# Three small reorderings in a float32 encoder kernel: a longer warm-up, low parts of probabilities last, and the last down-projection input split by parts

## The chip, the cores and the metric

The kernel runs on one core of a Trainium2 chip. The metric is device time in microseconds (us) of one execution; lower is better. The core's engines run at the same time and wait for each other through semaphores: TensorE (PE, matmuls into PSUM banks), VectorE (DVE), ScalarE (ACT), GpSimd (POOL), and the DMA queues, most of which SyncE (SP) issues. A matmul has a weight load (PEld) beside it.

## The reference, cut to what matters

A two-layer encoder over 512 tokens of width 1024 in float32. Layer 0 mixes tokens with gated linear attention, layer 1 with softmax attention; each is followed by a gated MLP of inner width 2816 with a width-3 convolution.

```python
def block(q_blk):
    s = jnp.einsum('bkgqd,bksd->bkgqs', q_blk, k).astype(jnp.float32) * scale
    p = jax.nn.softmax(s, axis=-1).astype(v.dtype)
    return jnp.einsum('bkgqs,bksd->bkgqd', p, v)

def conv_ffn(h, w_up, w_conv, b_conv, w_down):
    u = h @ w_up
    u = lax.conv_general_dilated(u, w_conv[:, None, :], window_strides=(1,), padding=[(1, 1)], ...) + b_conv
    val, gate = jnp.split(u, 2, axis=-1)
    return (jax.nn.silu(gate) * val) @ w_down

for i in range(DEPTH):
    h = rmsnorm(x, norm_mix[i])
    ...
    x = x + gla_mixer(h, ...)      # i = 0;  attn_mixer(h, ...) for i = 1
    x = x + conv_ffn(rmsnorm(x, norm_ffn[i]), ffn_w_up[i], ffn_w_conv[i], ffn_b_conv[i], ffn_w_down[i])
```

## The kernel before, in words

**Products in three parts.** TensorE multiplies in a rounded float32 format (fp32r). To keep float32 accuracy each operand is split into a high part (rounded by ScalarE, `activation(..., AF.Copy)`) and a low part (what rounding left, a subtraction on VectorE). A product is then three matmuls into one PSUM bank, in the helper `mm3(ps, wh, wl, mh, ml, ...)`: weight high by moving high, weight high by moving low, weight low by moving high. All matmuls go through `mm`, line 90 of the profile, so the profile tells them apart by the names of their tiles.

**Order of instructions.** A planner orders each engine's instructions ahead of time, by program order and its own estimate of when operands are ready; on the chip each engine then works its list in order and waits at semaphores. From the last block of an MLP's up-projection on (`pinned[0]`), the matmuls keep program order exactly. In the attention they do not: there the planner may put matmuls of one step between those of another.

**PSUM.** There are eight banks, in four groups that rotate: `acc` (3), `s` (2), `pt` (2), `po` (1). A tile that takes a bank waits until the last reader of the tile that had it is done.

**The start.** While the first weights and inputs are on their way, TensorE multiplies constants into a bank named `warm` (float32, 128 columns; each matmul leaves two records in the profile). Its first eight columns, all -0.5 after eight accumulated matmuls, are kept as `halfneg`. The first real matmuls are the tiles `vg`.

**Attention.** For each of 8 heads and each half of the queries (256), `turn` transposes two blocks of probabilities (tile `pt`, from `pr`) and splits them into `pth` (ScalarE) and `ptl` (VectorE). `mix` multiplies them with the values (`vh`, `vl`) for four blocks of keys into the bank `po`: twelve matmuls. The output projection (`op`, `out_stream`) and the next heads' query projections (`A`, `B`) are laid between the steps. `oT` is the split result of a head.

**The MLP's end.** The down-projection is done in six parts of the 22 inner blocks (`PARTS`, the last one of 3), each part adding into the residual `x` (line 900) one tile `dn` for each of the 8 row blocks of `x`. The inputs are the split gated activations `gu`: high at line 837 on ScalarE, low at line 838 on VectorE. The last part cannot end before the last `gu` is there, so its first tiles start early: each of 3 (first layer) or 4 (second layer) takes a bank from `LAST_BANKS` and multiplies its first two inputs, and only then comes the last input of each, with `finish`: the add into `x` and, in the first layer, the next norm's split of that row block (`xhl`, lines 357 and 362, and its square, 366 and 370), in the second the write to the output. The remaining tiles follow, one after the other, from bank `acc`. In the second layer the last row block ends in two halves, written by two queues (lines 889 to 895).

**Weights.** `Weights` converts weights ahead of their use into six buffers `w` (three pairs of high and low); a conversion waits until the last matmul that reads the old contents has passed. The first weights of the attention (`raw`, lines 171 and 173) are converted on ScalarE when a pair of the last down weights is free; their low part is finished by a DMA that adds (line 215). The first attention projection is the tile `A`, which reads `xhl` of all eight row blocks in order.

Of the kernel before, what the change touches and what calls it, by code (L numbers as in the profile page):

```python
# [15 lines left out]
P = 128  # L16
# [3 lines left out]
NT = S // P  # L20
# [3 lines left out]
QH, HD = 8, 128  # L24
# [21 lines left out]
FIRST_DMA = False  # L46
IN_TWO = ()
STEPS = 4
STEPS0 = 9
EARLY_INNER = (3,)  # L50
IN_BANKS = ("s", "s", "s", "acc")
AFTER = (False, False, False, True)
AT_TAG = 't'
LAST_BANKS = (("acc", "acc", "po"), ("acc", "acc", "s", "acc"))
SHARES1 = (2, 2, 2, 2)

PC_NORM = 0
# [7 lines left out]
def hybrid_encoder_kernel(  # L65
# [23 lines left out]
    def mm(*a, **k):  # L89
        i = pe.matmul(*a, **k)  # L90
        if pinned[0]:
            tc.keep_in_program_order(i)
# [13 lines left out]
    def bank(tag, n):  # L106
        return pp.tile([P, S], F32, tag=tag, bufs=PS[tag], name=nm(n))

    def pair(tag, bufs, dt, n):
        return sp.tile([P, 2 * S], dt, tag=tag, bufs=bufs, name=nm(n))  # L110

    def big(dt, n):
        return pair("g", 22, dt, n)
# [3 lines left out]
    def tmp(tag, n, w=S, dt=F32):  # L117
        pool_ = sp if tag == "sq" else stage[-1]
        return pool_.tile([P, w], dt, tag=tag, bufs={"u": 4, "t": 6, "sq": 3}[tag], name=nm(n))
# [183 lines left out]
    two = tmp("sq", "two")  # L303
    dve.memset(two[:, :P], 2.0 ** -5)
    dve.memset(two[:, P : 2 * P], -(2.0 ** -6))
    warm = bank("po", "warm")
    for i in range(8):
        mm(warm[:, :P], two[:, :P], two[:, P : 2 * P], start=i == 0, stop=i == 7)
    halfneg = cp.tile([P, 8], F32, name="halfneg")
    dve.tensor_copy(halfneg, warm[:, :8])  # L310
    ones = cp.tile([P, 1], F32, name="ones")
# [78 lines left out]
    def mm3(ps, wh, wl, mh, ml, start, stop, **k):  # L390

        mm(ps, wh, mh, start=start, stop=False, **k)
        mm(ps, wh, ml, start=False, stop=False, **k)
        mm(ps, wl, mh, start=False, stop=stop, **k)
# [368 lines left out]
    def ffn(layer, norm, cw, nxt):  # L763
        H = S // 2
        wide = lambda n: stage[-1].tile([P, 2 * S], F32, tag="w4", bufs=4, name=nm(n))
        hl, forms = [], {}
# [74 lines left out]
        def plain(m, part):  # L841
            u = wide("u")
            for t in range(2):
# [6 lines left out]
                elif m > 0:  # L850
                    for _ in range(STEPS):
                        next(building, None)
                if m == 0 and t == 1:
                    dve.tensor_tensor(u[:, :S], first, norm.R, ALU.mult)
                    dve.tensor_tensor(u[:, S:], ps, norm.R, ALU.mult)
                    for _ in range(STEPS0):
                        next(building, None)
# [41 lines left out]
        def finish(c, ps, last):  # L899
            dve.tensor_tensor(x[c], x[c], ps, ALU.add)  # L900
            if last and nxt is not None:
                nxt.chunk(c)
            elif last:
                sync.dma_start(out[c * P : (c + 1) * P, :], x[c])
# [48 lines left out]
        tiles = part_tiles(len(PARTS) - 1)  # L953
        k0, ends_ = sum(PARTS[:-1]), {}
        early = [(c, us, bank(tag, "dn")) for (c, us), tag in zip(tiles, LAST_BANKS[layer])]
        for late in (False, True):
            for c, us, ps in early:
                for i, u in enumerate(us):
                    if (i == len(us) - 1) != late:
                        continue  # L960
                    if u // 8 not in ends_:
                        ends_[u // 8] = W.half(down[layer], u // 8)
                    wh, wl = ends_[u // 8]
                    sl = slice((u % 8) * P, (u % 8 + 1) * P)
                    mm3(ps, wh[:, sl], wl[:, sl], *hl[k0 + i], i == 0, late)
                if late:
                    finish(c, ps, True)
        cur[0] = ends_[tiles[len(early) - 1][1][-1] // 8]
        for c, us in tiles[len(early):]:
# [3 lines left out]
    def attention(norm, nxt):  # L973
# [63 lines left out]
        def split(y, tile_):  # L1037
            act.activation(tile_[:, :S], y, AF.Copy)
            dve.tensor_tensor(tile_[:, S:], y, tile_[:, :S].bitcast(F32), ALU.subtract)
# [51 lines left out]
        ps = [bank("acc" if j < 2 else "pt", "av") for j in range(NT)]  # L1091
# [7 lines left out]
        vh, vl = big(F32R, "vh"), big(F32R, "vl")  # L1099
        for j in range(NT):  # L1100
            sl = slice(j * 256, (j + 1) * 256)
# [49 lines left out]
        def mix(h, hf):  # L1151
            ph3, pl3 = pts.pop((h, hf))
            vo = (h // 4) * HD
            if hf == 0:
                pos[h] = bank("po", "po")
            dst = pos[h][:, hf * 256 : (hf + 1) * 256]
            for k in range(NT):
                vsl = slice(k * 256 + vo, k * 256 + vo + HD)
                mm3(dst, vh[:, vsl], vl[:, vsl], ph3[:, k, :], pl3[:, k, :], k == 0, k == NT - 1)
            if hf == 1:  # L1160
                t = big(F32R, "oT") if h < 4 else pair("xhl", 8, F32R, "oT")
                split(pos[h], t)
                oh[h] = (t[:, :S], t[:, S:])
# [11 lines left out]
        for t in range(len(blocks) + LAG2):  # L1175
            if t < len(blocks):
                scores(*blocks[t])
            if 1 <= t <= len(blocks):
                copy(*blocks[t - 1])
            for g in plan[t]:  # L1180
                next(g, None)
            if LAG <= t < len(blocks) + LAG:
                turn(*blocks[t - LAG])
            if t < len(blocks):
                shares(*blocks[t])
            if t >= LAG2:
                h, j = blocks[t - LAG2]
                if j % 2 == 1:
                    mix(h, j // 2)
# [14 lines left out]
    with staged("ffn0"):  # L1204
        ffn(0, norms[1], cw, norms[2])
    with staged("att"):
        attention(norms[2], norms[3])
    with staged("ffn1"):
        ffn(1, norms[3], cw, None)
# [87 lines left out]
```

## Time and profile before

| | |
|---|---|
| median of 3 timed runs | 1103.08 us (1102.5, 1103.11, 1103.08) |
| the profiled execution's own time | 1100.86 us |
| its span, first to last instruction | 1099.1 us |
| TensorE busy | 1092.6 us (99%), 6530 matmul records |
| VectorE, ScalarE, GpSimd busy | 888.9 (81%), 620.2 (56%), 73.5 us (7%) |
| granted TensorE clock, mean of the span | 1.000 |

A row of the timeline gives the start in us, the busy time in us, the engine, the line, the operation, "out<-in", shapes and how many instructions were merged into the row (x2); in brackets stands how long the engine had been idle before it and who released it. Ends of matmuls are modelled, so the time that a matmul costs in a stream is read from the starts of its row and the next one, not from its duration. "Q" behind an engine (SPq) is its DMA issue.

### The profile page before, as it was taken

The numbers are of one execution on the slowest core, as the hardware profiler recorded it, in microseconds if no ns is written. First come the engines' busy times: TensorE is split into PE (matmuls) and PEld (weight loads), VectorE is DVE, ScalarE is ACT, GpSimd is POOL, SyncE is SP. The second block draws the span as 40 slices with busy tenths as digits, with TensorE's granted clock in tenths as the row PEclk, the third lists the DMA queues.
The fourth block names the chain that finished last, engine by engine and source line by source line (L and its number), as shares of the span: only waits on it lengthen the run. The fifth ranks groups of instructions, "written<-read, shape, count | busy, mean of one in ns | idle before, by whom it ended". The sixth has DMA issues, their size and how long they took to land.

```text
span 1099.1 us, 16431 instructions
## 1 busy us (share of the span) xinstructions
PE 1092.6 (99%) x6530; PEld 972.3 (88%) x6530; DVE 888.9 (81%) x1392; ACT 620.2 (56%) x913; POOL 73.5 (7%) x74
## 2 busy tenths in 40 slices
PE   9999999999999999999999999999999999999998
PEld 7888888888899999999988888888889999999997
DVE  6786675569999999979885567666999999997985
ACT  6478343467555545444464878956755454554441
POOL 0100000011000000000004334001100000000000
PEclk9999999999999999999999999999999999999999
DMA  6422221378323232323338754446733323232322
GB/s 223 148 93 77 77 100 65 118 163 191 123 104 116 96 116 77 126 69 113 124 91 201 180 161 122 159 146 163 189 120 111 116 96 115 78 121 72 116 77 77
DMA packets 31084, 132.72 MB, mean 121 GB/s; under 512 B 3616, under 2 KB 4128, under 8 KB 22304
## 3 DMA queue, kind: packets, MB, share of 16 engines
q1 hardware_dynamic: 20352, 102.16, 27.7%
q0 software_dynamic: 5184, 18.88, 8.9%
q10 hardware_dynamic: 5472, 10.64, 2.6%
q8 instruction: 51, 0.84, 0.3%
q14 instruction: 25, 0.20, 0.1%
HBM read 100.21 MB, written 2.10 MB: 93 GB/s over the span
## 4 chain that ended last, share of the span: by engine, by line
PE 93%; issue 3%; DMA 2%; DVE 1%; POOL 0%; ACT 0%; SPq 0%; POOLq 0%
PE dn L90 21%; PE Y L90 18%; PE X L90 13%; PE op L90 8%; PE vg L90 8%; PE up L90 5%; PE A L90 3%; PE B L90 3%; PE po L90 2%; PE s L90 2%; PE k L90 2%; PE q L90 2%; DMA wl<-raw 2%; PE o L90 1%; PE av L90 1%
## 5 line engine op out<-in xcount | busy, mean ns | idle before, releaser
L90 PE MATMUL dn<-gu,wh 128*128 128x512 f32 x708 | 218.6, 390 | 0.1
L90 PEld LDWEIGHTS dn<-gu,wh 128*128 128x128 f32 x708 | 130.3, 188 | 26.0 <-DVE x L900 1.0
L90 PE MATMUL dn<-gu,wl 128*128 128x512 f32 x354 | 137.4, 388 | 0.0
L830 ACT ACTIVATE y<-u,cw 128x512 f32<-128x512 f32 x88 | 67.8, 807 | 87.0 <-DVE u L934 75.0
L90 PE MATMUL X<-th,xwh 128*128 128x256 f32 x384 | 108.7, 283 | 0.0
L90 PE MATMUL X<-th,xwl 128*128 128x256 f32 x384 | 108.7, 283 | 0.0
L90 PE MATMUL X<-tl,xwh 128*128 128x256 f32 x384 | 108.7, 283 | 0.0
L171 ACT ACTIVATE wh<-raw 128x1024 fp32r<-128x1024 f32 x72 | 76.2, 1058 | 52.2 <-DVE raw L204 16.4
L90 PE MATMUL up<-xhl,wh 128*128 128x512 f32 x320 | 99.0, 390 | 0.0
L900 DVE TENSOR_TENSOR x<-x,dn 128x512 f32<-128x512 f32 x95 | 64.5, 682 | 31.3 <-PE dn L90 31.0
L171 ACT ACTIVATE wh<-draw 128x1024 fp32r<-128x1024 f32 x44 | 46.7, 1061 | 68.6 <-PE dn L90 46.0
L90 PE MATMUL vg<-wh,xhl 128*128 128x512 f32 x256 | 79.6, 390 | 1.1 <-DVE wh L223 1.1
L90 PE MATMUL Y<-th,wl 128*128 128x256 f32 x280 | 79.2, 283 | 0.0
L90 PE MATMUL Y<-th,wh 128*128 128x256 f32 x280 | 79.2, 283 | 0.0
L90 PE MATMUL Y<-tl,wh 128*128 128x256 f32 x280 | 79.2, 283 | 0.0
L90 PEld LDWEIGHTS dn<-gu,wl 128*128 128x128 f32 x354 | 66.5, 188 | 13.8
L90 PE MATMUL op<-oT,wh 128*128 128x512 f32 x256 | 76.9, 394 | 0.0
L90 PEld LDWEIGHTS X<-th,xwh 128*128 128x128 f32 x384 | 73.7, 192 | 0.5 <-DVE v L914 0.4
L90 PEld LDWEIGHTS X<-tl,xwh 128*128 128x128 f32 x384 | 73.7, 192 | 0.1
L90 PEld LDWEIGHTS X<-th,xwl 128*128 128x128 f32 x384 | 73.7, 192 | 0.0
L90 PEld LDWEIGHTS up<-xhl,wh 128*128 128x128 f32 x320 | 59.8, 188 | 12.2
L215 POOL DMA_DIRECT2D wl<-raw x36 | 31.6, 878 | 492.9 <-ACT wl L173 492.8
(249 smaller groups left out, 2861.3 us busy)
## 6 DMA issues: line engine op xcount, KB each, us to landing
raw<-in_w_up_dram SPq DMA_DIRECT2D x44, 1024.0 KB, 4.9
draw<-in_w_down_dram SPq DMA_DIRECT2D x44, 512.0 KB, 3.7
wl<-raw POOLq DMA_DIRECT2D x36, 512.0 KB, 5.0
pr<-p ACTq DMA_DIRECT2D x32, 256.0 KB, 2.5
raw<-in_w_vg_dram SPq DMA_DIRECT2D x6, 1024.0 KB, 4.9
raw<-in_w_akq_dram SPq DMA_DIRECT2D x5, 1024.0 KB, 6.3
raw<-in_w_kq_dram SPq DMA_DIRECT2D x4, 1024.0 KB, 4.9
raw<-in_w_gout_dram SPq DMA_DIRECT2D x4, 1024.0 KB, 4.9
```

Of the source, the lines that this page charges most:

```text
L90: i = pe.matmul(*a, **k)
L171: act.activation(hi, r, AF.Copy)
L215: pool.dma_start(dst, src, accum_op=ALU.add)
L830: act.activation(yt, ut, AF.Identity, scale=w(1), bias=w(3))
L900: dve.tensor_tensor(x[c], x[c], ps, ALU.add)
```

## The change

Three edits, and a new list of banks that goes with the third:

- **Warm-up.** `WARM = 2` more matmuls of constants ahead of the eight, each a group of its own, so 20 records instead of 16. The eight that give `halfneg` are the same.
- **`mix`.** The twelve matmuls of a half are the same, in another order: for each block of keys the two with the high part of the probabilities (`pth`), and after all blocks the four with the low part (`ptl`).
- **The MLP's end.** For the early down tiles the last input comes in two passes instead of one: first its high (rounded) part by both weight parts for all early tiles, then for each tile its low part by the high weights, and `finish`. The early tiles' banks change from `acc, acc, po` to `s, acc, po` (first layer) and from `acc, acc, s, acc` to `po, acc, acc, s` (second layer).

```diff
+WARM = 2
...
-LAST_BANKS = (("acc", "acc", "po"), ("acc", "acc", "s", "acc"))
+LAST_BANKS = (("s", "acc", "po"), ("po", "acc", "acc", "s"))
...
-    for i in range(8):
-        mm(warm[:, :P], two[:, :P], two[:, P : 2 * P], start=i == 0, stop=i == 7)
+    for i in range(-WARM, 8):
+        mm(warm[:, :P], two[:, :P], two[:, P : 2 * P], start=i <= 0, stop=i < 0 or i == 7)
...
-        for late in (False, True):
+
+        for late in range(3):
             for c, us, ps in early:
                 for i, u in enumerate(us):
-                    if (i == len(us) - 1) != late:
+                    if (i == len(us) - 1) != (late > 0):
                         continue
                     if u // 8 not in ends_:
                         ends_[u // 8] = W.half(down[layer], u // 8)
-                    wh, wl = ends_[u // 8]
                     sl = slice((u % 8) * P, (u % 8 + 1) * P)
-                    mm3(ps, wh[:, sl], wl[:, sl], *hl[k0 + i], i == 0, late)
-                if late:
+                    wh, wl, (mh, ml) = ends_[u // 8][0][:, sl], ends_[u // 8][1][:, sl], hl[k0 + i]
+                    if late == 0:
+                        mm3(ps, wh, wl, mh, ml, i == 0, False)
+                    elif late == 1:
+                        mm(ps, wh, mh, start=False, stop=False)
+                        mm(ps, wl, mh, start=False, stop=False)
+                    else:
+                        mm(ps, wh, ml, start=False, stop=True)
+                if late == 2:
                     finish(c, ps, True)
...
-            for k in range(NT):
-                vsl = slice(k * 256 + vo, k * 256 + vo + HD)
-                mm3(dst, vh[:, vsl], vl[:, vsl], ph3[:, k, :], pl3[:, k, :], k == 0, k == NT - 1)
+            vs = [slice(k * 256 + vo, k * 256 + vo + HD) for k in range(NT)]
+            todo = [(k, i) for k in range(NT) for i in range(2)] + [(k, 2) for k in range(NT)]
+            for n, (k, i) in enumerate(todo):
+                mm(dst, (vl if i == 1 else vh)[:, vs[k]], (pl3 if i == 2 else ph3)[:, k, :], start=n == 0, stop=n == 3 * NT - 1)
```

## The prediction

> **What bounds the kernel now.** I read the page's busy line and chain first, then the waits of TensorE alone, then the timeline at each place that the change touches.
>
> ```profile
> span 1099.1 us, 16431 instructions
> PE 1092.6 (99%) x6530; PEld 972.3 (88%) x6530; DVE 888.9 (81%) x1392; ACT 620.2 (56%) x913; POOL 73.5 (7%) x74
> PE 93%; issue 3%; DMA 2%; DVE 1%; POOL 0%; ACT 0%; SPq 0%; POOLq 0%
> PE vg L90 <- DVE wh L223: 1.1, 1, 1.1
> PE po L90 <- DVE ptl L1149: 0.5, 1, 0.5
> ```
>
> The first three lines are the page's: TensorE (PE) is busy in 1092.6 of 1099.1 us, and 93% of the chain that ended last is its own work. So the matmuls are the bound, and only about 6.5 us of the whole span is not matmul. The change removes no matmul (it adds four records at the start), so it can only win back small stalls. The last two lines are from PE's waits: the start, where it waits for the first converted weights, and one wait of the attention's last products for the low parts of probabilities (ptl). Stalls at PSUM banks have no line there; they show as gaps between matmul starts.
>
> The profiled execution took 1100.86 us, 1.8 above its span; the three timed runs have a median of 1103.08, 2.2 us above it. I make the sum against the profiled execution and apply its difference to the median. A difference of 0.2% (2.2 us) is about what a measurement of this kernel can tell from no change.
>
> **The change part by part.**
>
> *Attention.* The twelve products of a half were ordered high, low, high for each of four blocks, so the second needed ptl. Now the eight with high parts come first.
>
> ```profile
> 701.25 0.45 PE L1145 MATMUL pt<-ident,pr 128*128 128x128 f32 x4
> ...
> 702.31 0.27 PE L90 MATMUL po<-pth,vh 128*128 128x256 f32 x1
> 703.04 0.38 PE L90 MATMUL po<-ptl,vh 128*128 128x256 f32 x1 [0.46 <-DVE ptl L1149]
> 703.27 0.28 PE L90 MATMUL po<-pth,vl 128*128 128x256 f32 x1
> 703.38 0.28 PE L90 MATMUL po<-pth,vh 128*128 128x256 f32 x1
> ...
> 705.51 0.45 PE L1145 MATMUL pt<-ident,pr 128*128 128x128 f32 x4
> ...
> 702.31 0.68 DVE L1149 TENSOR_TENSOR ptl<-pt,pth 128x512 fp32r<-128x512 f32 x1
> ...
> 704.25 0.68 DVE L1149 TENSOR_TENSOR ptl<-pt,pth 128x512 fp32r<-128x512 f32 x1
> ```
>
> Products of 256 columns start every 0.12 us (703.27 to 703.38). The second came 0.73 after the first, 0.61 too late, and the third 0.23 after that, 0.11 too late: 0.72 us lost. VectorE delivers ptl at 702.31 + 0.68 = 702.99. In the new order it is needed 8 x 0.12 = 0.96 us after 702.31, at 703.27, so the stall goes whole. What is late next: PE would reach the transposes of 705.51 at 704.79, and they write the bank of the transposes two before (the two banks alternate, so that of 701.25), which VectorE has read only at 704.25 + 0.68 = 704.93. With the 0.05 that VectorE's end at 702.99 lay before PE's start at 703.04, that is 704.98, and with up to 0.11 of refill 705.09: 0.2 to 0.3 us given back. I take 0.25, so a gain of 0.47 (ends: 0.72, nothing given back; 0, if the other interleaving of products and output projection brings a like wait). Behind the attention the output projection and the next up-projection are matmuls back to back, so what is left goes through. The other fifteen halves show no such wait, so for them the order costs and gains nothing.
>
> *End of the first layer's MLP.* Three early down tiles took banks acc, acc, po; now s, acc, po. The high parts of the last input are multiplied for all three tiles first, the rounded (low) part last.
>
> ```profile
> 557.66 0.39 PE L90 MATMUL dn<-gu,wl 128*128 128x512 f32 x1
> 558.12 0.74 PE L90 MATMUL dn<-gu,wh 128*128 128x512 f32 x2
> 558.70 0.40 PE L90 MATMUL dn<-gu,wl 128*128 128x512 f32 x1
> 558.93 0.63 PE L90 MATMUL dn<-gu,wh 128*128 128x512 f32 x2
> ...
> 561.01 0.73 PE L90 MATMUL dn<-gu,wh 128*128 128x512 f32 x2
> 561.59 0.40 PE L90 MATMUL dn<-gu,wl 128*128 128x512 f32 x1
> 561.82 0.62 PE L90 MATMUL dn<-gu,wh 128*128 128x512 f32 x2
> ...
> 557.38 0.68 DVE L900 TENSOR_TENSOR x<-x,dn 128x512 f32<-128x512 f32 x1
> ...
> 559.83 0.63 ACT L837 ACTIVATE gu<-y 128x512 fp32r<-128x512 f32 x1 [1.75 <-DVE y L835]
> ...
> 560.50 0.69 DVE L838 TENSOR_TENSOR gu<-y,gu 128x512 fp32r<-128x512 f32 x1
> ```
>
> A 512-column matmul starts every 0.23 us (558.70 to 558.93). The second tile's first starts 0.46 after its forerunner: its acc bank is read by the add at line 900 until 557.38 + 0.68 = 558.06. That is 0.23 lost, and 0.12 more as the pair takes 0.58 instead of 0.46. With s for the first tile the second gets the acc bank a tile older, so 0.35 goes. At 561.01 the pair again takes 0.12 too long: low gu is ready at 560.50 + 0.69 = 561.19 and was wanted at 561.24, less its passing on. Now six high products (1.36 us) precede it. High gu is ready at 559.83 + 0.63 = 560.46, before PE's new arrival at 560.66. PE is then 0.47 us ahead. But it does not stay so:
>
> ```profile
> 562.48 1.06 ACT L171 ACTIVATE wh<-raw 128x1024 fp32r<-128x1024 f32 x1 [2.02 <-PE dn L90]
> ...
> 565.14 0.75 DVE L362 SCALAR_TENSOR_TENSOR xhl<-x,prm,xhl 128x512 fp32r<-128x512 f32 x1 [1.06 <-ACT xhl L357]
> ...
> 575.95 0.68 DVE L900 TENSOR_TENSOR x<-x,dn 128x512 f32<-128x512 f32 x1
> ...
> 577.42 0.75 DVE L362 SCALAR_TENSOR_TENSOR xhl<-x,prm,xhl 128x512 fp32r<-128x512 f32 x1 [0.79 <-ACT xhl L357]
> ...
> 578.15 0.63 PE L90 MATMUL A<-xhl,wh 128*128 128x512 f32 x2
> ```
>
> ScalarE's conversion at 562.48 waits for the weight buffer that the second tile reads last. Before, the last reader of that buffer is the second matmul of 561.82, at 562.05; now it is the eighth of the late ones, seven starts of 0.227 after 560.66, at 562.25: 0.2 us later, not earlier. Behind this conversion stand the next layer's first high part and, from 565.14, VectorE's low parts, which fill it without a gap until the last add of the residual (575.95); then the last low part ends at 577.42 + 0.75 = 578.17, and PE uses it 0.24 after 578.15. So there is about 0.2 us between the two, and none that PE could come forward into. I take the whole 0.47 as given back in a new wait of the first attention projection (tile A) near 578: 0 for this part. Ends: -0.47 (if the conversions come in another order), +0.2 (if the chain is 0.2 later to its end).
>
> *End of the second layer's MLP.* Four early tiles, banks now po, acc, acc, s.
>
> ```profile
> 1080.05 0.39 PE L90 MATMUL dn<-gu,wl 128*128 128x512 f32 x1
> 1080.51 0.73 PE L90 MATMUL dn<-gu,wh 128*128 128x512 f32 x2
> 1081.08 0.39 PE L90 MATMUL dn<-gu,wl 128*128 128x512 f32 x1
> ...
> 1093.77 0.69 DVE L900 TENSOR_TENSOR x<-x,dn 128x512 f32<-128x512 f32 x1 [1.35 <-PE dn L90]
> ```
>
> The same bank wait: 0.46 instead of 0.23, then 0.57 instead of 0.46, 0.34 lost and now won. No next layer follows, and VectorE waits 1.35 us for PE before the late adds (last row), so the end moves with PE. The four adds come later and closer together, and their writes queue on SP, but 8 us before the last one. -0.34 (ends: -0.34, and -0.23 if a refill stays).
>
> *Warm-up.* Two more matmuls of fp32, two records each, sixteen to twenty.
>
> ```profile
> 1.30 3.51 PE L90 MATMUL warm<-two 128*128 128x128 f32 x16 [1.30 <-DVE bd L314]
> 5.93 1.15 PE L90 MATMUL vg<-wh,xhl 128*128 128x512 f32 x4 [1.13 <-DVE wh L223]
> L90 PE MATMUL warm<-two x7: 421/421/422, 1.7 to 3.0; 128*128 128x128 f32 x7
> L90 PE MATMUL warm<-two x2: 274/274/275, 4.4 to 4.5; 128*128 128x128 f32 x2
> ```
>
> Seven records start from 1.7 to 3.0, one every 0.21 us; by 4.4 they have become shorter (274 ns instead of 421), so the clock rose during the burst. Four more records at the early pace are 0.85 us, and 1.30 + 3.51 + 0.85 = 5.66 is before 5.93, where PE waits for the weights anyway. They cost 0. If the cover went (weights there at once), they would cost up to 0.85. After 5.93 the first matmuls run at the full rate (four in 1.15 us), so in this execution a longer burst gains nothing either.
>
> Sum: -0.47 + 0 - 0.34 + 0 = -0.81 us; from all ends -1.53 to -0.03. That puts the profiled execution at 1100.05 and the median at **1102.3**.
>
> **The rivals.**
>
> *The warm-up is the main thing.* The timed runs lie 2.2 us above the profiled execution. If in them the clock had not risen within the burst, the first real matmuls would run at half speed, and 4.4 us of that, to about 10.3, cost 2.2. In the profile the clock rose some 3 us into unbroken work. The short burst is followed by 1.1 us of idle time before 5.93; with 20 records at the slow pace only 0.3 us stays idle, so the work is as good as unbroken from 1.30 on and the clock would rise within twice 3 us, by 7.3: at most 1.4 us at half speed are left, 0.7 lost instead of 2.2. That gives back 1.5 to 2.2 us: 1100.1 to 1100.8, say 1100.5. For it: the size fits, and the clock in the profile rose only at the burst's very end. Against: the three runs lie within 0.6 us of each other, which a matter of chance need not give, and a constant offset between timed and profiled runs does as well. The Trainium skill ("TensorE: Matmul & The Clock Gate", Part 1) says the same from the other side: the gate opens after about 3.4 us of sustained activity, judged in a free-running window, so that the same kernel can start with more or fewer cold matmuls. By that rule a burst of 3.51 us opens it in some runs only, and an estimate from the page's window would be that a longer burst wins one to two microseconds in the others; the trace, with one opening at 4.2 to 4.4 us, agrees but can't show the others.
>
> *The other interleaving in the attention costs more than it saves.* TensorE's order there is the planner's, and products that no longer wait for ptl take other places between the output projection's matmuls. One wait like that at 703.04 costs 0.72. Each half could meet one, at a transpose's bank still being read (shown above, 0.25) or at ptl. Two new ones of 0.72, with the old one gone and 0.34 won elsewhere, give 1103.08 + 1.44 - 0.72 - 0.34 = 1103.5; from two on it is slower than before, from five on by over 0.2%. Against: only one of sixteen halves shows a wait now, and the new order asks for the late operand later in each.
>
> *The first layer's gain is kept.* If ScalarE takes the residual's first chunk before the weights, VectorE's chain starts earlier and the 0.47 stays: 1101.8.
>
> **How the numbers follow.** Likeliest, the sum: 0.47 chance, 1102.3, of its own range 1101.5 to 1103.1. First layer's gain kept: 0.13, 1101.8. Warm-up: 0.30, 1100.5, of which three quarters lie beyond -0.2% (1100.9), since the cold time may be shorter than 4.4 us. Worse interleaving: 0.10, from 1103.1 up, of which half passes +0.2% (1105.3). So faster 0.23, same 0.72, slower 0.05. The range takes in the warm-up case down to 1099.7 and the mild losses up to 1103.8.
>
> **What would show it.** Right: the row of po waiting for ptl is gone; the gaps before the second early down tiles (at 558 and 1080) are gone; a new gap of about half a microsecond in tile A at 578, with VectorE's last low part as its releaser; four more warm records and the first vg matmul still at 5.9. The forecast is wrong if the timed runs fall by over 2 us while the profiled execution falls by one, if tile A shows no gap, or if other halves of the attention begin to wait.

## The result, and the profile after

The changed kernel takes 1100.22 us (median of 12 runs, 1099.6 to 1100.91) against 1103.09 for the kernel before on the same chip (12 runs, 1101.32 to 1103.4, eleven of them above 1102.4). The ratio is 0.9976 with a 95% interval of 0.9967 to 0.9985: 2.87 us less, in an interval from 1.7 to 3.6 us. Zero lies outside it, but its lower end is below the 2.2 us that the prediction took as what a measurement can tell from none.

The two profiled executions say something else. Theirs are 1100.86 us before and 1100.91 after, with the same span of 1099.1 us. So the first thing to explain is why a kernel that is 2.87 us faster over its timed runs shows no gain in its profile. First lines of the page after, and two rows of TensorE's waits:

```profile
span 1099.1 us, 16436 instructions
PE 1093.7 (100%) x6534; PEld 973.8 (89%) x6534; DVE 888.1 (81%) x1392; ACT 619.7 (56%) x913; POOL 73.5 (7%) x74
PE 94%; issue 3%; DMA 2%; POOL 1%; ACT 0%; DVE 0%; POOLq 0%
PE warm L91 <- DVE bd L315: 1.3, 1, 1.3
PE up L91 <- DMA wl<-raw: 0.7, 1, 0.7
```

The wait for ptl is gone from the list, and so is the 1.1 us wait of the first vg matmul. A wait of an up-projection matmul for weights that a DMA finishes is now long enough to be listed. TensorE's busy time rose by 1.1 us, as much as the burst of constants grew: 4.64 us below, against 3.51 before.

The gain can be followed by asking, place by place, how late the same matmul of the stream starts after against before. TensorE's timeline of the kernel before, rows not shown yet:

```profile
6.92 1.07 PE L90 MATMUL vg<-wl,xhl 128*128 128x512 f32 x4
11.68 0.39 PE L90 MATMUL vg<-wl,xhl 128*128 128x512 f32 x1
270.84 0.50 PE L90 MATMUL up<-xhl,wl 128*128 128x512 f32 x1
793.26 0.50 PE L90 MATMUL up<-xhl,wl 128*128 128x512 f32 x1
1095.56 0.28 PE L90 MATMUL dn<-gu,wl 128*128 128x256 f32 x1
```

The same places in the changed kernel:

```profile
1.30 4.64 PE L91 MATMUL warm<-two 128*128 128x128 f32 x20 [1.30 <-DVE bd L315]
5.91 1.86 PE L91 MATMUL vg<-wh,xhl 128*128 128x512 f32 x4
7.61 1.08 PE L91 MATMUL vg<-wl,xhl 128*128 128x512 f32 x4
12.39 0.39 PE L91 MATMUL vg<-wl,xhl 128*128 128x512 f32 x1
272.24 0.50 PE L91 MATMUL up<-xhl,wl 128*128 128x512 f32 x1 [0.74 <-DMA wl<-raw]
559.05 0.39 PE L91 MATMUL dn<-gu,wl 128*128 128x512 f32 x1
702.12 0.46 PE L1153 MATMUL pt<-ident,pr 128*128 128x128 f32 x4
793.68 0.50 PE L91 MATMUL up<-xhl,wl 128*128 128x512 f32 x1
1081.17 0.39 PE L91 MATMUL dn<-gu,wl 128*128 128x512 f32 x1
1095.63 0.28 PE L91 MATMUL dn<-gu,wl 128*128 128x256 f32 x1
```

| place | before | after | how late | step |
|---|---|---|---|---|
| vg, the 26th matmul | 11.68 | 12.39 | +0.71 | start: +0.71 |
| up-projection, layer 1 | 270.84 | 272.24 | +1.40 | landing of weights: +0.69 |
| early down tiles, layer 1 | 557.66 | 559.05 | +1.39 | |
| transposes in the attention | 701.25 | 702.12 | +0.87 | end of the first MLP: -0.52 |
| up-projection, layer 2 | 793.26 | 793.68 | +0.42 | attention: -0.45 |
| early down tiles, layer 2 | 1081.08 | 1081.17 | +0.09 | second MLP's banks: -0.33 |
| last matmul of tile dn shown | 1095.56 | 1095.63 | +0.07 | |

So the reorderings won 0.52 + 0.45 + 0.33 = 1.30 us in this execution, and 1.40 us were lost ahead of them in two places that no reordering touches. At the start, four vg matmuls took 7.61 - 5.91 = 1.70 us instead of 6.92 - 5.93 = 0.99: the clock rose only at 7.42 us here (at 4.38 in the profile before; both from the trace's record of the granted clock), and (7.42 - 5.91) / 2 = 0.75 is what half speed until then costs. At 271 us the wait for the DMA was 0.69 longer than before. Two single executions can differ by more than the change is worth; the ladder shows what the change itself did. It repeats: from the down tiles at 558 to the last one at 1096 the profile above gains 1.39 - 0.07 = 1.32 us, a second profile of the changed kernel (on chip B, below) 1.26, and the one with the reorderings but 16 records 1.50.

Against the timed 2.87 us the reorderings leave about 1.6 us that the two profiles can't show.

### The profile page after: what moved, and what is told of

It is laid out like the page before. It is cut to its first block, busy times and chain, and to the rows that moved or that the text cites. A ratio compares the mean times of both kernels' runs of the same rounds, so it can differ in the third digit from the quotient of the medians.

```text
span 1099.1 us, 16436 instructions
## 1 busy us (share of the span) xinstructions
PE 1093.7 (100%) x6534; PEld 973.8 (89%) x6534; DVE 888.1 (81%) x1392; ACT 619.7 (56%) x913; POOL 73.5 (7%) x74
## 4 chain that ended last, share of the span: by engine, by line
PE 94%; issue 3%; DMA 2%; POOL 1%; ACT 0%; DVE 0%; POOLq 0%
PE dn L91 22%; PE Y L91 18%; PE X L91 13%; PE op L91 8%; PE vg L91 8%; PE up L91 5%; PE A L91 3%; PE B L91 3%; PE s L91 2%; PE po L91 2%; PE k L91 2%; PE q L91 2%; DMA wl<-raw 2%; PE o L91 1%; PE av L91 1%
```

## The experiments

Two questions were open. **What won the other 1.6 us:** the longer burst, because the clock rises late in many timed runs of the kernel before (my theory then), or the reorderings, with the start playing no part (the rival)? **Why was the gain of the first layer's end kept**, which I had given back in full: do the new banks bring it, or the split passes, or only both? Each kernel ran 11 times with its profile, beside 33 runs of the kernel before on its chip. There were three chips: A (before: median 1101.50, mean 1101.71), B (1102.78, 1102.35) and C (1101.61, 1101.92). All are the kernel before plus the edit shown, unless they start from the changed one.

### The start

**Only the warm-up of 20 records**, on chip A.

```diff
-    for i in range(8):
+    for i in range(-2, 8):   # start=i <= 0, stop=i < 0 or i == 7
```

> The kernel before with the 20 warm-up records alone. Clock theory (in most runs of the kernel before the TensorE clock is still low when the first vg matmuls start): 1.2 to 1.8 us below the kernel before, 1101.3 to 1101.9, and in its profile the vg matmuls run at the full rate (0.23 us each) from 8.0 us on at the latest. Rival, a constant offset between the profiled execution and the timed runs: no change, 1103.1. Stalls of attention and down tiles stay as they were (0.72, 0.47 and 0.34 us).

Measured: median 1101.42, mean 1101.44, 1100.72 to 1102.14; ratio 0.9997 [0.9988, 1.0006]. The gain of 1.2 to 1.8 us that I had expected did not come: 0.08 us in the median and 0.27 in the mean, neither clear of no change. On this chip the kernel before itself lies 1.6 us lower than in the first comparison. What differs is the spread: the 33 runs of before reach from 1100.68 to 1103.37, eight of them above 1102.3; of the 11 here none is.

**The changed kernel with 16 records**, on chip A.

```diff
-WARM = 2
+WARM = 0
```

> The changed kernel with 16 warm-up records: reorderings alone. Clock theory: the three stalls that its trace no longer has, less the one it has gained, 0.48 + 0.47 + 0.34 = 1.3 us below the kernel before, 1101.8, and runs spread over 2 us or more, as with the kernel before. Rival (the warm-up does nothing): the whole 2.9 us, 1100.2.

Measured: 1100.35, mean 1100.59, 1098.95 to 1102.68; ratio 0.9989 [0.9980, 0.9998]. The mean is 1.12 below before: close to the 1.30 of the ladder. With 16 records the runs spread over 3.7 us, so the interval is wide, 0.2 to 2.2 us; it holds the ladder's figure and excludes the rival's 2.9.

**The changed kernel again**, on chip B, no edit.

> The changed kernel once more, on the chip of this call. Clock theory (the clock's rise falls on a grid of its own, so the kernel before has a spread of 3 us and the level depends on the chip's phase): 1.2 to 1.6 us below the kernel before by median, with a spread under 1.5 us. Rival, the first ratio holds everywhere: 2.9 below.

Measured: 1100.13, mean 1100.16, 1099.19 to 1101.03; ratio 0.9980 [0.9971, 0.9989]. Here the 33 runs of before fall into two groups with nothing between them: 13 from 1100.59 to 1101.49 (mean 1101.02) and 20 from 1102.55 to 1103.98 (mean 1103.22). The distance is 2.2 us. The changed kernel has one group, 1.8 us wide, and lies 2.65 below by the median and 2.19 by the mean: more than the 1.2 to 1.6 that I had expected, nearer the 2.9 of the first comparison.

**A burst of 8 records**, on chip B, four matmuls of a doubled constant.

```diff
-    dve.memset(two[:, P : 2 * P], -(2.0 ** -6))
+    dve.memset(two[:, P : 2 * P], -(2.0 ** -5))
...
-    for i in range(8):
+    for i in range(4):   # stop=i == 3
```

> The kernel before with 8 warm-up records (four matmuls of twice the value), ending near 3.2 us. Theory A and B alike: the clock never rises within the warm-up, so every run pays 1.5 to 3 us: 1102.2 to 1104, none under 1101.8; vg matmuls at 0.43 us each until 9 to 12 us. Offset theory: as the kernel before.

Measured: 1103.48, mean 1103.24, 1102.41 to 1104.23; ratio 1.0010 [1.0001, 1.0019]. All runs lie about where the upper group of before lies. TensorE's timeline at the start, first of this kernel:

```profile
1.29 2.08 PE L90 MATMUL warm<-two 128*128 128x128 f32 x8 [1.29 <-DVE bd L314]
5.76 2.05 PE L90 MATMUL vg<-wh,xhl 128*128 128x512 f32 x4 [2.39 <-DVE wh L223]
7.60 1.91 PE L90 MATMUL vg<-wl,xhl 128*128 128x512 f32 x4
9.31 2.94 PE L90 MATMUL vg<-wh,xhl 128*128 128x512 f32 x8
```

and of the kernel with 16 records and the new order of `mix` (below), whose profiled execution took 1103.10 us:

```profile
1.30 3.79 PE L90 MATMUL warm<-two 128*128 128x128 f32 x16 [1.30 <-DVE bd L314]
5.90 2.04 PE L90 MATMUL vg<-wh,xhl 128*128 128x512 f32 x4 [0.81 <-DVE wh L223]
7.74 1.91 PE L90 MATMUL vg<-wl,xhl 128*128 128x512 f32 x4
9.45 2.19 PE L90 MATMUL vg<-wh,xhl 128*128 128x512 f32 x8
```

The first eight vg matmuls take 3.55 us in both instead of 1.9: the clock rose at 11.33 and at 9.82 us. The 26th vg matmul starts at 14.14 and 13.51 there, against 11.68 in the profile before. So the late clock that the prediction held to be possible exists with 16 records too, and the execution shown is the longest of that kernel's 11. With 20 records or more the latest rise in any profile was 7.42.

**16 records, started later**, on chip B. Seven fills of the constant go ahead, so that the burst should end when the weights come.

```diff
+    for _ in range(7):
+        dve.memset(two[:, P : 2 * P], -(2.0 ** -6))
```

> The kernel before with 16 warm-up records that start 0.8 to 0.9 us later (seven fills of the constant instead of one), so that they end at about 5.7, right ahead of the vg matmuls. Theory A, the gap between warm-up and vg is what loses the clock: spread of at most 2 us, nothing over 1102.6, and a profile whose clock rises by 8.5 us. Theory B, the amount of warm-up work counts: as the kernel before, spread of 2.7 us or more, some runs over 1102.8.

```profile
2.96 3.78 PE L90 MATMUL warm<-two 128*128 128x128 f32 x16 [2.96 <-DVE two L306]
6.40 1.89 PE L90 MATMUL vg<-wh,xhl 128*128 128x512 f32 x4
```

Measured: 1102.65, mean 1102.50, 1101.68 to 1103.5; ratio 1.0001 [0.9993, 1.0010]. The burst started at 2.96 and not near 2.1, as a fill took 0.24 us, and it held vg back to 6.40. Two signs of theory A came, a spread of 1.8 us and a rise of the clock before 8.5 (at 7.97); the third did not, as six of the 11 runs lie above 1102.6. The level didn't fall. In the profile the start explains about 1.25 us of that: vg half a microsecond late, and (7.97 - 6.40) / 2 = 0.78 at half speed. The experiment was mis-sized and settles little.

**28 records**, on chip B, the changed kernel with `WARM = 6`.

> The changed kernel with 28 warm-up records. They are 1.7 us longer than 20 at the slow rate, past the 5.2 to 6.0 at which the weights come: vg starts at 6.0 to 7.3, while the clock gains nothing more than with 20. 0.3 to 0.9 us slower than the changed kernel. Theory that more warm-up is always better: faster than the changed kernel by 0.2 to 0.5.

```profile
1.29 5.74 PE L91 MATMUL warm<-two 128*128 128x128 f32 x28 [1.29 <-DVE bd L315]
6.79 1.17 PE L91 MATMUL vg<-wh,xhl 128*128 128x512 f32 x4
```

Measured: 1100.96, mean 1101.36; ratio 0.9992 [0.9983, 1.0001]; 0.83 above the changed kernel on the same chip. The cover that made four records free ends here: vg starts at 6.79 instead of 5.76 to 5.91. Twenty are long enough and not yet too long, of the four lengths tried. Not all of the 0.83 need come from the burst: three of the 11 runs lie above 1102.3, and the profiled one of them (1102.35) had its clock up at 6.25 but lost 1.28 us more than the profile before at the second layer's up-projection, where a matmul at 794.75 had waited 1.36 us for weights from a DMA.

### The reorderings, one by one

First without the longer burst, on chip A: only the new order of the twelve products in `mix`, and only the MLP's end (banks and split passes).

> The kernel before with the new order of attention's products alone. Prediction's term: 0.47 us below, 1102.6 (0.72 won at the first low product of the twelfth half, 0.25 given back at the next transposes). Rival, other interleaving costs more: above 1103.1 with new gaps between the matmuls of 630 to 725 us.

> The kernel before with banks and split passes at both MLP ends alone. By the changed kernel's trace: 0.47 at the first layer's end kept, since VectorE adds the last row block together with the one before it, and 0.34 at the second's: 0.81 below, 1102.3. Prediction's term (first layer given back near 578): 0.34 below, 1102.7, with a gap in tile A.

Measured: 1101.08, mean 1101.44, ratio 0.9997 [0.9988, 1.0006]; and 1101.59, mean 1101.29, ratio 0.9997 [0.9989, 1.0006]. Both keep the wide spread of 16 records (3.2 and 3.6 us), which buries terms of half a microsecond. The traces do not: in the first the wait for ptl is gone and 0.23 us appears at the next transposes, in the second the gaps at 558, 561 and 1080 are gone and tile A of the next layer runs without a gap.

So I took the terms apart with 20 records as the common base, all on chip C: that base, the base with only the new banks, with only the split passes, and with only the new `mix`.

```diff
+LAST_BANKS = (("s", "acc", "po"), ("po", "acc", "acc", "s"))   # banks only
+        for late in range(3):   # split only, the loop as in the change
```

> The kernel before with 20 warm-up records, as the base for the next three: 1101.2 to 1101.6 with a spread under 1.6 us, one hump instead of the kernel before's two.

> 20 records and the new banks alone. My theory (banks and split need each other in the first layer): the gap at the second early tile goes at both ends, but in the first layer PE then meets the low part of gu 0.35 us earlier and waits that much longer for it, so only the second layer's 0.34 is won: 0.34 below the base. Rival (the two are independent): 0.35 + 0.34 = 0.7 below the base.

> 20 records and the split passes alone, old banks. The gaps of 0.34 to 0.35 at the second early tile stay at both ends; only the 0.11 us wait for the low part of gu goes in the first layer: 0.1 below the base. VectorE adds the last row block of x right behind the one before, as in the changed kernel, and tile A has no gap. If the late finish cost something by itself, it would show here: above the base.

> 20 records and the new order of attention's products alone: 0.48 below the base (0.72 won near 703, 0.24 given back at the next transposes), and tile A and the down tiles as in the kernel before.

| kernel | median | mean | range | ratio to before |
|---|---|---|---|---|
| 20 records | 1101.07 | 1101.14 | 1100.46 to 1101.91 | 0.9994 [0.9985, 1.0003] |
| and banks | 1101.35 | 1101.32 | 1100.05 to 1101.8 | 0.9996 [0.9987, 1.0005] |
| and split passes | 1101.25 | 1101.65 | 1100.57 to 1103.52 | 0.9995 [0.9986, 1.0004] |
| and `mix` | 1101.31 | 1101.05 | 1099.79 to 1102.03 | 0.9996 [0.9987, 1.0004] |

No time differs from another by more than its uncertainty. Three of the 11 runs with the split passes lie above 1102.3, although the kernel has 20 records; the others with 20 have none. What the traces show is clear all the same. With banks only, TensorE at the end of the first layer's early tiles:

```profile
561.78 0.42 PE L90 MATMUL dn<-gu,wh 128*128 128x512 f32 x1
562.42 0.50 PE L90 MATMUL dn<-gu,wh 128*128 128x512 f32 x1 [0.22 <-DVE gu L838]
562.76 0.39 PE L90 MATMUL dn<-gu,wl 128*128 128x512 f32 x1
```

The gap at the second early tile is gone, but the second matmul of the last input now comes 0.64 us after the first instead of 0.23, and the next 0.34 after it: 0.41 + 0.11 = 0.52 us are lost waiting for low gu, where before it was 0.11. TensorE arrives 0.35 earlier and waits 0.41 longer. In the first layer the banks alone win nothing.

With the split passes alone, TensorE in both layers, and VectorE's adds in the second:

```profile
557.60 0.39 PE L90 MATMUL dn<-gu,wl 128*128 128x512 f32 x1
558.06 0.73 PE L90 MATMUL dn<-gu,wh 128*128 128x512 f32 x2
...
1086.35 1.90 PE L90 MATMUL dn<-gu,wh 128*128 128x512 f32 x6
1088.09 0.40 PE L90 MATMUL dn<-gu,wl 128*128 128x512 f32 x1
...
1086.78 2.48 DVE L900 TENSOR_TENSOR x<-x,dn 128x512 f32<-128x512 f32 x4 [3.39 <-PE dn L90]
```

The bank gap stays (0.46 from 557.60 to 558.06), the wait for low gu is gone, and in the second layer a new one appears that I had not expected: the six matmuls from 1086.35 take 1.74 us to the next start instead of 6 x 0.227 = 1.36, so 0.38 more. The fifth tile takes an acc bank there whose add comes only after the late passes (from 1086.78). Each half of the edit leaves a wait that the other half removes: the split needs the banks in the second layer, and the banks need the split in the first.

## Why the prediction was right or wrong

The forecast was 1102.3, of a range from 1099.7 to 1103.8; the measured 1100.22 is in the range, 2.1 us below the forecast. It came out as the rival "the warm-up is the main thing" (chance 0.30, 1100.5) together with "the first layer's gain is kept" (0.13). That the range holds it is owed to the rival: the range of the sum itself began at 1101.5. Three of the four terms hold in the traces, but two signs that the prediction had named against itself came: tile A has no gap, and the timed runs fell by over 2 us while the profile hardly moved.

**Attention: right.** 0.72 was to be won and 0.25 given back at the next transposes. One row of TensorE before, then TensorE's and VectorE's rows after:

```profile
704.75 0.93 PE L90 MATMUL s<-k,q 128*128 128x512 f32 x3
...
703.18 0.28 PE L91 MATMUL po<-pth,vh 128*128 128x256 f32 x1
703.29 0.28 PE L91 MATMUL po<-pth,vl 128*128 128x256 f32 x1
...
704.13 0.64 PE L91 MATMUL po<-ptl,vh 128*128 128x256 f32 x4
704.61 0.45 PE L1153 MATMUL pt<-ident,pr 128*128 128x128 f32 x4
704.90 0.93 PE L91 MATMUL s<-k,q 128*128 128x512 f32 x3
705.90 0.51 PE L1153 MATMUL pt<-ident,pr 128*128 128x128 f32 x4
...
705.12 0.68 DVE L1157 TENSOR_TENSOR ptl<-pt,pth 128x512 fp32r<-128x512 f32 x1
```

The twelve products run without a gap from 703.18, the four with ptl last. The second transposes start 1.00 after the s products of 704.90, where before the step from 704.75 to 705.51 was 0.76, and their bank is free at 705.12 + 0.68 = 705.80: 0.24 given back. No other half shows a new wait, so the rival of a worse interleaving fell.

**Second layer's end: right.** The stall of 0.34 is gone, 0.33 by the ladder, in the rows around 1080; VectorE's later adds and the writes delayed nothing (the last matmul of tile dn keeps the +0.07 of the ladder).

**First layer's end: the step that gave everything back was wrong.** The 0.47 at 558 and 561 was won as worked out, but no wait of tile A near 578 took it back.

```profile
561.77 0.39 PE L91 MATMUL dn<-gu,wl 128*128 128x512 f32 x1
562.00 0.42 PE L91 MATMUL dn<-gu,wh 128*128 128x512 f32 x1
562.26 0.40 PE L91 MATMUL dn<-gu,wl 128*128 128x512 f32 x1
...
562.73 0.39 PE L91 MATMUL dn<-gu,wl 128*128 128x512 f32 x1
...
578.39 0.62 PE L91 MATMUL A<-xhl,wh 128*128 128x512 f32 x2
578.85 0.39 PE L91 MATMUL A<-xhl,wl 128*128 128x512 f32 x1
579.07 0.62 PE L91 MATMUL A<-xhl,wh 128*128 128x512 f32 x2
...
563.15 1.06 ACT L172 ACTIVATE wh<-raw 128x1024 fp32r<-128x1024 f32 x1 [1.29 <-PE dn L91]
...
574.87 1.28 DVE L901 TENSOR_TENSOR x<-x,dn 128x512 f32<-128x512 f32 x2
...
578.21 0.75 DVE L363 SCALAR_TENSOR_TENSOR xhl<-x,prm,xhl 128x512 fp32r<-128x512 f32 x1
```

Two links of the chain that I had built failed. I had ScalarE's conversion wait for the buffer that the second tile reads in the eighth late matmul, 1.59 us into the late phase. It starts at 563.15, 1.15 after that phase's start at 562.00, right behind the end of the fourth late matmul (562.73 + 0.39 = 563.12). By this timing it takes the buffer of the low weights, which the split passes leave first; before, it came 562.48 - 561.01 = 1.47 in. And I had held VectorE's chain to be fixed in its order, with the last add of the residual as its last but one link. The planner made another: the adds of the last two row blocks run together at 574.87, ahead of the low parts that fill the chain's end. The last low part ends at 578.21 + 0.75 = 578.96 and TensorE needs it about 579.30, so the margin is still 0.3 us with TensorE 0.47 further ahead; I had 0.2 without that and none with it. A split alone brings the same new order, banks alone keep the old one: I had copied the old order into a kernel whose operands are ready at other times. The term was 0 and measured -0.47 at the two places, -0.52 up to the attention.

**Warm-up: right in the profile, wrong for the timed runs.** Four more records delayed nothing in the profile: vg starts at 5.91 after against 5.93 before. The step that failed is the last of the sum: I carried the difference of 2.2 us between the profiled execution and the median over to the changed kernel, as if it were the same for every run. For the changed kernel it is -0.7 (1100.22 against 1100.91). The profile before was an execution of the lower sort; eleven of the twelve runs beside it were not. In the profiles the late clock is shown as a cause: half speed until it rose put the start off by 1.8 and 2.5 us, and the 8-record kernel lies wholly at the upper level. In the timed runs it is inferred, from the two groups 2.2 us apart: they record only the mean clock of the span, 0.999 or 1.000, and the profile whose clock rose at 9.82 has 1.000 too. The rival's own estimates were near what the profiles show: a rise about 10.3 with 16 records (measured 9.82 and 9.93 in the late ones) and by 7.3 with 20 (7.42 at the latest). The sizes agree roughly too. If the runs above 1102.3 (8 of 33, 9 of 33, 20 of 33, 11 of 12) each cost 2.2 us, then the burst alone is worth 0.5, 0.6, 1.3 and 2.0 us on average. Measured with the burst alone were 0.27 and 0.78 on the first two chips, and with the reorderings' 1.12 added the estimate for the last two is 2.5 and 3.1, against 2.19 and 2.69 (means; the medians of the last differ by 2.87). A rival for some of the long runs is the late landing of weights, which cost 1.28 us in the profile with 28 records; what made three runs with 20 records and split passes long wasn't recorded. Why the share differs so much from chip to chip stays open.

## What to carry to other kernels

One profile is one execution: where the timed median and the profiled time differ, find out what differs before a sum is carried from one to the other, and compare two kernels by how late the same instruction starts, place by place, rather than by their spans. A burst that warms the clock should last until the first real work can start, no shorter and no longer: 16 records that ended about a microsecond early left the start to chance, 20 had the clock up by 7.42 us in all seven profiles, and 28 delayed the work. When operands change their ready times, expect a planner to change the order of the engines behind them; edits that each leave a wait which the other removes have to be judged together.

## What the runs showed of the hardware

**The granted clock follows a fixed grid of its own.** In all 14 profiles the time from the clock's rise to its fall at the end is a whole number of windows of 3.4133 us: 1095.678 us, 321.0 of them, before; 320.0 after; 319.0 with 16 records and the new orders. Where the grid lies against the kernel's start differs from execution to execution: the rise came at 4.38 and 7.42 in the two first profiles, between 4.42 and 7.28 in the others with 20 records or more, and between 4.38 and 9.93 with 16 that start at 1.30. In the window that ended at the rise TensorE was in matmuls for 0.90 (before) to 1.0 of the time; the fullest windows that raised nothing were filled to 0.72, 0.75, 0.76 and 0.79. So in these profiles the bound lies between 0.79 and 0.90, if a window ends where the clock rises. That is how an idle gap ahead of vg counts: the windows that held the gaps of 0.97 and 0.81 us (16 records, rises at 9.93 and 9.82) were filled to 0.72 and 0.76, and the next chance was a window later. With 20 records the burst reaches 5.3 to 5.9, and by this bound no rise should come after about 7.8: a window that misses holds at least a tenth of idle time ahead of 1.30, so it began by 0.96, and the next one ends two windows of 3.41 after that. The latest seen is 7.42.

The Trainium skill ("TensorE: Matmul & The Clock Gate", Part 1) describes such a window, 3413 ns long, free-running, and says that the first matmuls of the same kernel therefore run cold in varying number. The grid of 3.4133 us and the varying rise agree.

**A DMA that finishes weights lands at times that vary.** At 271 us the up-projection waits for weights that an adding DMA finishes. That cost 0.34 us in the profile before, 1.01 after, nothing with the split passes alone and 1.15 in the control with 20 records, whose code there is the same:

```profile
270.16 0.61 PE L90 MATMUL up<-xhl,wh 128*128 128x512 f32 x2
271.66 0.50 PE L90 MATMUL up<-xhl,wl 128*128 128x512 f32 x1 [0.88 <-DMA wl<-raw]
```

From 270.16 to 271.66 are 1.50 us, where two matmuls take 0.46; the other 0.11 is lost in the refill behind it. At the like place of the second layer the profile with 28 records lost 1.28 us more than the profile before. What makes the landing early or late wasn't tried and stays open; it is part of the spread of 1.3 to 1.8 us that even kernels with one group of times have.
